# Parameter chain of the S5 layer one feed-forward earlier, its tables spread over the second, and other PSUM banks in both mixers

## The chip, the cores and the metric

The kernel runs on one core of a Trainium2 chip. A time is the device time of one execution, in microseconds; of several runs the median is given. The core has five engines with a queue each: TensorE (PE) multiplies matrices into eight PSUM banks, VectorE (DVE), ScalarE (ACT) and GpSimd (POOL) work on rows of 128 partitions, and SyncE (SP) issues the large transfers. Each queue runs in the order of the program and stops at an instruction whose operands aren't there.

## The reference

A decoder trunk of two layers on x of 256 positions by 1024. Each layer is a half-step SwiGLU, a mixer and another half-step SwiGLU, each behind an RMS norm:

```python
x = x + 0.5 * swiglu(rmsnorm(x, g0), w_gate, w_up, w_down)   # inner width 2816
x = x + mixer(rmsnorm(x, g1))
x = x + 0.5 * swiglu(rmsnorm(x, g2), w_gate, w_up, w_down)
```

The first layer's mixer is a gated spatial MLP (u, v of 512 columns each, v normed by head and mixed over positions) beside sparse attention of 8 heads (compressed, selected and windowed keys, mixed by sigmoid gates). The second layer's mixer is causal pooling beside a diagonal state-space layer (S5) of 32 groups with 64 states. What the change moves is the preparation of that layer, which depends on parameters alone:

```python
dt      = exp(log_dt)
lam_bar = exp((lam_re + 1j * lam_im) * dt)
b_bar   = ((lam_bar - 1) / lam)[..., None] * (b_re + 1j * b_im)
# states_t = lam_bar * states_{t-1} + b_bar u_t;  y = Re(c states) + d u
```

## The kernel before, in words

**Stages.** One pass in program order, in us of the profiled span: first feed-forward about 24 to 212, even mixer to 335, second feed-forward to 530, third to 722, odd mixer to 802, fourth to 1003. Activations lie with features on partitions, so a product has a weight tile as its stationary operand and 256 positions as the moving one. Each float32 weight is split into a rounded high half `wh` (ScalarE, L97) and a rest `wl` (VectorE, L98), and each product takes three matmuls: `wh` by the high half of the activation, `wl` by it, and `wh` by its low half.

**Weights.** They stream through three raw buffers of two units (a unit is 128 by 1024). `used()` marks a unit as consumed by TensorE and at once issues the split of the unit six further on. So the `wl` of a coming unit stands in VectorE's queue between the chains of the present ones, and a late VectorE makes weights late.

**A feed-forward** `ffn(f, after)` has 22 inner tiles j. A step of its loop from index 3 is: the `jobs` hung on (f, j), the projection of tile j (`proj`, 48 matmuls into `gu`, L125 to L132), `chain(j)` and the down projection of tile j-1 (24 matmuls into `y`, L114 to L116). `chain(j)` goes back and forth: `e` on VectorE (L252), `s` on ScalarE (L255), `h` on VectorE (L257), `hh` on ScalarE (L260), the low half `hl` on VectorE (L261). The projection of j+1 covers the chain of j; the last down projection follows the one before it directly. At its end `after` adds each PSUM block into x (L738) and sums squares for the next norm on GpSimd.

**Jobs** are how work of other stages gets into a feed-forward: `put(f, j0, per, todo)` hangs a list on the steps from j0, so many to a step. They are issued in program order, but GpSimd runs its own queue as fast as operands allow; only a copy called `pace` (L289), which reads `hl` of index 2, holds GpSimd back until the loop begins. Before, the jobs are:
- first feed-forward: the loads of the even mixer's constants (`even_loads`, L699), one on each step, on GpSimd's queue without a pace;
- second: the S5 parameter chain of `odd_prep` (helpers `tt`, L775, and `ts`, L779 and L781: small GpSimd instructions of 32 to 256 columns in scratch `sq`; two of its steps, a cast (L814) and a reciprocal (L861), are on VectorE, made by `with_vector`), 22 on a step; then, on the last ten steps, ten entries of the list `late`;
- third: the rest of `late`, two on a step, and in step 3 and after also the transposes `turn_w`, then the products `taps`, `cols`, `diag`, `bounce` and `phase`.

A table of `late` is one `mul2`: two products and a sum of 128 by 512 on GpSimd. Two make `bbar`, eight make `wtw`; then two scalings, a load of the C parameters, and nine more into `vt`.

**The even mixer** projects kk, q0, q1 in turn. `rope(b, o)` rotates each (four `zs`, L311, and a `zc`, L312, on VectorE, their sum on GpSimd). Then v in four units, into banks 7 and 4, and three units of narrow columns (`n`, L155: values and gate logits) into banks 6 and 5, with the attention scores of block n issued behind block n (`scores`; their row maxima are `am` on VectorE, L549, and their exponentials `pr` on ScalarE, L553, and `mu`, L347, is the mean of v's gelu). Then come twelve turns: each transposes one block of probabilities (`pt`, L571), and two or three pieces of other projections stand between as fill.

**The odd mixer** ends in `out_steps`, which accumulates the result in four banks: y[0], y[1] in 6 and 0, y[2], y[3] in 7 and 4. The first gate tile of a feed-forward is in bank 4, the next in 5 and 6.

## Time and profile before

| what | value |
|---|---|
| runs | 1007.43 us median of three, 1005.06 to 1009.93 |
| profiled execution | 1004.76 us, its span 1003.0 us |
| TensorE | busy 974.5 us, 97% |
| VectorE | busy 688.3 us, 69% |
| ScalarE | busy 477.9 us, 48% |
| GpSimd | busy 314.9 us, 31% |
| HBM read | 172 MB, 174 GB/s over the span |

An engine's busy time is the sum of its instructions in the profile; what ended an idle stretch ("releaser") is inferred from semaphores. A row of a timeline begins with start and length in us, and ends with the idle time before it and its releaser; a row of the list of windows has start and end, length, the busy time and count of TensorE's matmuls, its weight loads, VectorE, ScalarE and GpSimd, then the granted TensorE clock, the transfer engines' share and GB/s. GpSimd's work is not even: 166 of its us lie in the second feed-forward, 104 in the third, 8 in the first.

### The profile page before, as it was taken

What the parts mean: (1) busy time and instruction counts of PE and PEld (TensorE: products, weight loads), DVE (VectorE), ACT (ScalarE), POOL (GpSimd) and SP (SyncE); (2) the same over time, 40 slices, a digit from 0 to 9 for tenths busy, and PEclk for the clock granted to TensorE, in tenths of its full rate; (3) what the DMA queues carried; (4) which work ended last, traced back from release to release, by engine and by line L of the source; (5) the groups of instructions that cost most, each with busy time, mean ns of one, the idle gap of its engine ahead of it and who ended that gap; (6) DMA issues with size and microseconds to landing.
All of it is one profiled execution on the core that took longest, in us unless ns stands there. A gap on an engine that the chain in (4) does not pass through costs nothing.

```text
span 1003.0 us, 19482 instructions
## 1 busy us (share of the span) xinstructions
PE 974.5 (97%) x8171; PEld 952.8 (95%) x8171; DVE 688.3 (69%) x949; ACT 477.9 (48%) x728; POOL 314.9 (31%) x441
## 2 busy tenths in 40 slices
PE   8999999998999999999989999999999999999997
PEld 7999999998887999999989999999998999999997
DVE  6766556697774776648788788566788676656563
ACT  6544444455454564435435535444465555444442
POOL 3100000012120259999992495329510000000001
PEclk9999999997999999999998999999999999999999
DMA  8855454534212565535542745559452436554521
GB/s 280 341 210 184 180 188 173 202 138 157 85 43 84 177 247 180 188 123 198 209 167 86 273 142 184 193 181 284 173 169 119 177 133 246 191 188 175 204 85 42
DMA packets 32856, 175.48 MB, mean 175 GB/s; under 512 B 7792, under 2 KB 10032, under 8 KB 12928
## 3 DMA queue, kind: packets, MB, share of 16 engines
q1 hardware_dynamic: 29696, 166.21, 46.2%
q0 software_dynamic: 2496, 7.41, 2.4%
q8 instruction: 64, 1.05, 0.4%
q10 hardware_dynamic: 576, 0.62, 0.2%
q14 instruction: 24, 0.20, 0.1%
HBM read 172.12 MB, written 2.10 MB: 174 GB/s over the span
## 4 chain that ended last, share of the span: by engine, by line
PE 75%; POOL 9%; DVE 8%; issue 4%; ACT 3%; DMA 1%; SPq 1%; ACTq 0%; POOLq 0%; DVEq 0%
PE gu L125 13%; PE gu L127 13%; PE gu L132 13%; PE y L114 8%; PE y L116 8%; PE y L115 8%; POOL sq L775 4%; DVE wl L98 4%; POOL sq L779 3%; PE sc L541 1%; PE oT L486 1%; DMA raw<-in_ws 1%; DVE zs L311 1%; PE pt L571 1%; ACT wh L97 1%
## 5 line engine op out<-in xcount | busy, mean ns | idle before, releaser
L98 DVE TENSOR_TENSOR wl<-raw,wh 128x1024 fp32r<-128x1024 f32 x308 | 394.9, 1316 | 121.0 <-ACT wh L97 120.9
L125 PE MATMUL gu<-xh,wh 128*128 128x256 f32 x1408 | 365.5, 282 | 3.6 <-DVE x L738 2.6
L127 PE MATMUL gu<-xh,wl 128*128 128x256 f32 x1408 | 364.2, 282 | 0.6 <-DVE wl L726 0.3
L97 ACT CAST wh<-raw 128x1024 fp32r<-128x1024 f32 x308 | 311.3, 1048 | 105.4 <-PE gu L132 46.8
L132 PE MATMUL gu<-xl,wh 128*128 128x256 f32 x1408 | 275.9, 281 | 0.0
L125 PEld LDWEIGHTS gu<-xh,wh 128*128 128x128 f32 x1408 | 265.9, 189 | 5.8 <-issue 3.5
L127 PEld LDWEIGHTS gu<-xh,wl 128*128 128x128 f32 x1408 | 265.0, 188 | 1.9 <-DVE wl L726 1.7
L132 PEld LDWEIGHTS gu<-xl,wh 128*128 128x128 f32 x1408 | 213.8, 188 | 0.0
L114 PE MATMUL y<-hh,wh 128*128 128x256 f32 x704 | 199.0, 283 | 7.7 <-ACT hh L260 7.7
L116 PE MATMUL y<-hl,wh 128*128 128x256 f32 x704 | 199.4, 283 | 0.0
L115 PE MATMUL y<-hh,wl 128*128 128x256 f32 x704 | 199.2, 283 | 0.0
L255 ACT ACTIVATE s<-e 128x256 f32<-128x256 f32 x88 | 36.8, 418 | 234.7 <-DVE e L252 234.7
L114 PEld LDWEIGHTS y<-hh,wh 128*128 128x128 f32 x704 | 133.6, 190 | 8.3 <-ACT hh L260 8.3
L116 PEld LDWEIGHTS y<-hl,wh 128*128 128x128 f32 x704 | 133.4, 190 | 0.6 <-DVE hl L261 0.6
L115 PEld LDWEIGHTS y<-hh,wl 128*128 128x128 f32 x704 | 133.6, 190 | 0.0
L197 POOL TENSOR_TENSOR sq<-sq 128x512 f32<-128x512 f32 x10 | 13.6, 1360 | 292.4 <-ACT sq L195 224.5
L257 DVE TENSOR_TENSOR h<-s,e 128x256 f32<-128x256 f32 x88 | 49.5, 562 | 48.6 <-ACT s L255 48.6
L252 DVE TENSOR_TENSOR e<-gu,rb 128x512 f32<-128x512 f32 x88 | 60.5, 688 | 31.8 <-PE gu L132 30.2
L261 DVE TENSOR_TENSOR hl<-h,hh 128x256 fp32r<-128x256 f32 x88 | 41.9, 476 | 41.7 <-ACT hh L260 41.7
L747 POOL TENSOR_SCALAR sq<-x,gw 128x256 f32<-128x256 f32 x4 | 3.6, 918 | 187.0 <-DVE x L738 187.0
L260 ACT CAST hh<-h 128x256 fp32r<-128x256 f32 x88 | 35.8, 407 | 55.3 <-DVE h L257 55.3
L775 POOL TENSOR_TENSOR sq<-sq 128x64 f32<-128x64 f32 (+1 forms) x122 | 53.8, 461 | 4.0 <-DVE sq L814 0.3
(330 smaller groups left out, 1183.9 us busy)
## 6 DMA issues: line engine op xcount, KB each, us to landing
raw<-in_ws SPq DMA_DIRECT2D x154, 1024.0 KB, 4.9
toep<-kd POOLq DMA_DIRECT2D x8, 256.0 KB, 12.3
raw<-in_ws SPq DMA_DIRECT2D x4, 256.0 KB, 4.3
raw<-in_ws SPq DMA_DIRECT2D x2, 512.0 KB, 7.8
w<-in_w POOLq DMA_DIRECT2D x1, 1024.0 KB, 9.9
bnd<-in_bnd POOLq DMA_DIRECT2D x1, 544.0 KB, 9.2
x<-in_x SPq DMA_DIRECT2D x4, 128.0 KB, 3.6
x<-in_x SPq DMA_DIRECT2D x2, 256.0 KB, 7.1
```

The source lines that it names most:

```text
L97: S.copy(h, src)
L98: V.tensor_tensor(lo, src, h.bitcast(F32), op=OP.subtract)
L114: P.matmul(o, h, ah, start=first, stop=False, skip_group_check=True)
L115: P.matmul(o, lo, ah, start=False, stop=False, skip_group_check=True)
L116: P.matmul(o, h, al, start=False, stop=last, skip_group_check=True)
L125: P.matmul(os, h[:, c], xh[:, 4 * half + k], start=half == 0 and k == 0 and s == 0, stop=False, skip_group_check=True)
L127: P.matmul(os, lo[:, c], xh[:, 4 * half + k], start=False, stop=False, skip_group_check=True)
L132: P.matmul(o[:, T * s:T * s + T], h[:, c], xl[:, 4 * half + k], start=False, stop=half == 1 and k == 3, skip_group_check=True)
L252: V.tensor_tensor(e, gu[j].rearrange("p (a b) -> p a b", a=2), rb[:, None, :].to_broadcast([128, 2, T]), op=OP.mult)
L257: V.tensor_tensor(h, s, e[:, 1], op=OP.mult)
L261: V.tensor_tensor(hl[j], h, hh[j].bitcast(F32), op=OP.subtract)
L775: steps.append(lambda: G.tensor_tensor(o, p, q, op=op))
```

## The change

- The parameter chain hangs on the first feed-forward, 15 steps to a loop step instead of 22, in the same list as the even mixer's loads, and there is a `pace` copy in each of the first three feed-forwards. Its inputs `prm` and `sgn` are loaded at the start, and what it leaves (`pw`, `turn8`) lies in a pool that lives through the kernel; two results that lay in the scratch are now `turn8[3]` and `turn8[4]`.
- `late` hangs on the second feed-forward: ten entries on steps 3 to 7, three on step 8, nine on steps 10 to 18. `turn_w` is there from step 10; `cols`, `taps`, `diag`, `bounce` and `phase` are earlier in the third.
- In the even mixer the narrow block goes to banks 2 and 3, the scores n-1 follow block n, the sum of `rope(2)` is on VectorE, and v has four units of two input tiles by 512 columns, where it had two units of four input tiles for each half of 256 columns.
- In the odd mixer the banks of y[1] and y[3] change places, and the products into `yp` are in two halves with the second pooling between.

```diff
 
 def even_units():
     return (pair_units("kk", "q0") + pair_units("q1")
-            + [("v", b, k) for b in range(2) for k in range(2)] + [("n", k) for k in range(3)]
+            + [("v", k) for k in range(4)] + [("n", k) for k in range(3)]
             + pair_units("cc") + pair_units("u0") + pair_units("u1")
             + [("eo", d, k) for d, k in ((0, 0), (0, 1), (1, 0), (1, 1), (0, 2), (1, 2), (0, 3), (1, 3))])
 
...
         down(1)
         used()
         for j in range(3, NM):
-            if (f, j) in ((1, 3), (2, 3)):
+            if j == 3 and f < 3:
                 G.tensor_copy(pace, hl[j - 1].bitcast(F32)[:, 0:1])
             for job in jobs.get((f, j), ()):
                 job()
...
                 r = slice(32 * (q ^ 1), 32 * (q ^ 1) + 32)
                 V.tensor_tensor(v2(zs[32 * q:32 * q + 32]), v2(o)[r], cs[r, 1:2, :].to_broadcast([32, 2, T]), op=OP.mult)
             V.tensor_tensor(v2(zc), v2(o), cs[:, 0:1, :].to_broadcast([128, 2, T]), op=OP.mult)
-            G.tensor_tensor(roped[:, 2 * b:2 * b + 2], v2(zs), v2(zc), op=OP.add)
+            (V if b == 2 else G).tensor_tensor(roped[:, 2 * b:2 * b + 2], v2(zs), v2(zc), op=OP.add)
 
         o = [bank(4, "kk"), bank(5, "q0"), bank(6, "q1")]
         opening([("kk", o[0]), ("q0", o[1])])
...
 
         vps = [bank(7, "v0"), bank(4, "v1")]
 
-        def vblock(b, kh):
-            h, lo = unit(("v", b, kh))
-            for k in range(4):
-                c = slice(256 * k, 256 * k + 256)
-                kk = 4 * kh + k
+        def vblock(n):
+            h, lo = unit(("v", n))
+            for kk in (2 * n, 2 * n + 1):
+                c = slice(512 * (kk % 2), 512 * (kk % 2) + 512)
                 for t in range(2):
-                    mmn(vps[t][:, 256 * b:256 * b + 256], xh[:, kk, 128 * t:128 * t + 128],
-                        xl[:, kk, 128 * t:128 * t + 128], h[:, c], lo[:, c], kk == 0 and b == 0, kk == 7)
+                    mmn(vps[t], xh[:, kk, 128 * t:128 * t + 128], xl[:, kk, 128 * t:128 * t + 128], h[:, c], lo[:, c],
+                        kk == 0, kk == 7)
             used()
 
-        vblock(0, 0)
+        vblock(0)
         rope(1, o[1])
-        vblock(0, 1)
+        vblock(1)
         rope(2, o[2])
-        vblock(1, 0)
-        vblock(1, 1)
+        vblock(2)
+        vblock(3)
         gv = gm.tile([128, 8, 2, 64], F32, name="gv")
         for t in range(2):
             S.activation(gv[:, :, t], vps[t].rearrange("p (h d) -> p h d", d=64), AF.Gelu_apprx_tanh, scale=rc[:, t:t + 1])
...
             for _ in range(n):
                 next(fill, None)
 
-        nps = [bank(6, "n0"), bank(5, "n1")]
+        nps = [bank(2, "n0"), bank(3, "n1")]
         for n in range(3):
             h, lo = unit(("n", n))
             for k in range(NKS[n], NKS[n + 1]):
...
                         h[:, c], lo[:, c], k == 0, k == 7)
             if n < 2:
                 used()
-                scores(n)
+            if n:
+                scores(n - 1)
         V.tensor_scalar(hrc, rc, 0.5, None, op0=OP.mult)
         for t in range(2):
             V.tensor_scalar(vn[:, t], nps[t][:, 0:256], rc[:, t:t + 1], None, op0=OP.mult)
...
-        cr, ci = small(), small()
+        cr, ci = turn8[:, 3], turn8[:, 4]
...
         ts(turn8[:, 1], ui, sgn, OP.mult, -1.0, OP.mult)
         ts(pi, pi, sgn, OP.mult)
 
+        def put(f, j0, per, todo):
+            for i, t in enumerate(todo):
+                jobs.setdefault((f, j0 + i // per), []).append(t)
+
+        parts.append(steps)
+        j0, per = 3, 15
+        for part in parts:
+            put(0, j0, per, part)
+            j0 += -(-len(part) // per)
+        yield
+
         b1, b2 = bq[:, 0], bq[:, 1]
         g3 = lambda z: z.rearrange("p (g c) -> p g c", g=32)
         wide = lambda z: z[:, :, None].to_broadcast([128, 32, 16])
...
             late.append(lambda n=n: mul2(vt[:, :, n - 1] if n else vt0, g3(tw["c"][:, 0]), pr[:, n], g3(tw["c"][:, 1]), pi[:, n],
                                          OP.subtract))
 
-        def put(f, j0, per, todo):
-            for i, t in enumerate(todo):
-                jobs.setdefault((f, j0 + i // per), []).append(t)
-
-        parts.append(steps)
-        j0, per = 3, 22
-        for part in parts:
-            put(1, j0, per, part)
-            j0 += -(-len(part) // per)
-        put(1, NM - 10, 1, late[:10])
-        put(2, 3, 2, late[10:])
+        put(1, 3, 2, late[:10])
+        put(1, 8, 3, late[10:13])
+        put(1, 10, 1, late[13:])
 
         def turn_w(q):
             p = bank(7, "wt")
...
         scan(0)
         run(z3)
         yp = [bank(1, "yp"), bank(2, "yp")]
-        for g in range(32):
-            P.matmul(quad(yp, g), ub[:, g], tw["t"][:, g], start=g // 4 % 4 == 0, stop=False, skip_group_check=True)
-        pooled(1)
-        y = [bank(6, "y"), bank(0, "y"), None, None]
+        for hb in range(2):
+            for g in range(16 * hb, 16 * hb + 16):
+                P.matmul(quad(yp, g), ub[:, g], tw["t"][:, g], start=g // 4 % 4 == 0, stop=False, skip_group_check=True)
+            if not hb:
+                pooled(1)
+        y = [bank(6, "y"), bank(4, "y"), None, None]
 
         def out_steps(h2, k, first, last, done=None):
             h, lo = unit(("oo", h2, k))
...
         mixed_low(1, o2)
         scan(1)
         at["hold"] = False
-        y[2:] = [bank(7, "y"), bank(4, "y")]
+        y[2:] = [bank(7, "y"), bank(0, "y")]
         run(o00)
         carry(0)
         run(out_steps(1, 0, True, False))
...
+    prm = cst.tile([128, 3, 32], F32, name="prm")
+    sgn = cst.tile([128, 1], F32, name="sgn")
+    pw = cst.tile([128, 2, 9, 32], F32, name="pw")
+    turn8 = cst.tile([128, 5, 32], F32, name="turn8")
     even_loads()
+    for t_, n_ in ((prm, "prm"), (sgn, "sgn")):
+        nc.gpsimd.dma_start(t_, a[n_])
+    prep = odd_prep()
+    next(prep)
     ffn(0, step(1, 0.5))
     even(step(2, 1.0))
-    prm = ovp.tile([128, 3, 32], F32, name="prm")
-    sgn = ovp.tile([128, 1], F32, name="sgn")
-    pw = ovp.tile([128, 2, 9, 32], F32, name="pw")
-    turn8 = ovp.tile([128, 3, 32], F32, name="turn8")
...
     uu = ovp.tile([128, 32, 128], F32, tag="uu", name="uu")
     kk = ovp.tile([128, 2, 4, 128], F32, tag="kk", name="kk")
     odd_open()
-    odd_prep()
+    next(prep, None)
     ffn(1, step(3, 0.5))
     ffn(2, step(4, 0.5))
     odd(step(5, 1.0))
```

GpSimd at the first feed-forward: before, after the first norm's sum, the loads of the even mixer.

```order
L731 TENSOR_TENSOR sq<-sq 128x512 [waits Activation_49,Pool_49]
L699 DMA rot<-in_rot 128x128
L699 DMA cs<-in_cs 128x512
L699 DMA cse<-in_cse 128x64
L699 DMA neg<-in_neg 128x128
L699 DMA mc<-in_mc 128x32
```

After:

```order
L731 TENSOR_TENSOR sq<-sq 128x512 [waits Activation_49,Pool_49]
L1250 DMA prm<-in_prm 128x96
L1250 DMA sgn<-in_sgn 128x1
L289 COPY pace<-hl 128x1 [waits DVE_49]
L779 TENSOR_SCALAR sq<-prm 128x32 [waits DMASW0_49,PE_49]
L779 TENSOR_SCALAR sq<-sq 128x32 [waits Pool_49] x2
L781 TENSOR_SCALAR sq<-sq 128x32 [waits Pool_49]
```

The loads, which ran off at the start, now stand behind the pace and between the steps of the chain, the first of them some dozen steps behind it. (Rows of after carry its own line numbers.)

GpSimd at the second feed-forward, from the pace on: before, the first steps of the chain.

```order
L289 COPY pace<-hl 128x1 [waits DVE_49]
L779 TENSOR_SCALAR sq<-prm 128x32 [waits DMASW5_49,PE_49]
L779 TENSOR_SCALAR sq<-sq 128x32 [waits Pool_49] x2
L781 TENSOR_SCALAR sq<-sq 128x32 [waits Pool_49]
L779 TENSOR_SCALAR sq<-sq 128x32 [waits Pool_49]
L775 TENSOR_TENSOR sq<-sq,prm 128x32 [waits PE_49,Pool_49]
```

After, the tables (`bq` holds the B parameters, `gt` is the scratch of `mul2`):

```order
L289 COPY pace<-hl 128x1 [waits DVE_49]
L923 TENSOR_TENSOR gt<-bq,turn_198 128x512 [waits DMASW7_49]
L924 TENSOR_TENSOR gt<-bq,turn_198 128x512
L925 TENSOR_TENSOR bbar<-gt 128x512 [waits Pool_49]
L923 TENSOR_TENSOR gt<-bq,turn_198 128x512 [waits Pool_49]
L924 TENSOR_TENSOR gt<-bq,turn_198 128x512
L925 TENSOR_TENSOR bbar<-gt 128x512 [waits Pool_49]
```

Instructions of 512 columns stand where those of 32 were, and they wait for nothing but one load and one another.

VectorE in the even mixer, from the last rotation to the second maximum: before,

```order
L312 TENSOR_TENSOR zc<-q_2441,cs 128x512 [waits Pool_49]
L98 TENSOR_TENSOR wl<-raw,wh 128x1024 [waits DMAHW4_49,Activation_49]
L98 TENSOR_TENSOR wl<-raw,wh 128x1024 [waits Activation_49]
L347 TENSOR_REDUCE mu<-gv 128x16 [waits Activation_49]
L348 TENSOR_SCALAR mu<-mu 128x16 [waits DVE_49]
L98 TENSOR_TENSOR wl<-raw,wh 128x1024 [waits DMAHW5_49,PE_49,Activation_49]
L549 TENSOR_REDUCE am<-sc 128x4 [waits PE_49]
L550 TENSOR_SCALAR am<-am 128x4 [waits DVE_49]
L98 TENSOR_TENSOR wl<-raw,wh 128x1024 [waits Activation_49]
L549 TENSOR_REDUCE am<-sc 128x4 [waits PE_49]
```

After:

```order
L312 TENSOR_TENSOR zc<-q_2686,cs 128x512 [waits Pool_49]
L313 TENSOR_TENSOR roped<-zs,zc 128x512 [waits DVE_49]
L98 TENSOR_TENSOR wl<-raw,wh 128x1024 [waits DMAHW4_49,Activation_49]
L98 TENSOR_TENSOR wl<-raw,wh 128x1024 [waits Activation_49]
L346 TENSOR_REDUCE mu<-gv 128x16 [waits Activation_49]
L347 TENSOR_SCALAR mu<-mu 128x16 [waits DVE_49]
L98 TENSOR_TENSOR wl<-raw,wh 128x1024 [waits DMAHW5_49,PE_49,Activation_49]
L98 TENSOR_TENSOR wl<-raw,wh 128x1024 [waits Activation_49]
L548 TENSOR_REDUCE am<-sc 128x4 [waits PE_49]
L549 TENSOR_SCALAR am<-am 128x4 [waits DVE_49]
L548 TENSOR_REDUCE am<-sc 128x4 [waits PE_49]
```

The sum of the last rotation stands ahead of the two `wl`, and the first maximum has moved behind the second of the `wl` that stood on both sides of it.

## The prediction

> **What bounds the kernel now.** First the page's totals, then TensorE's own waits, then the stretches in which its clock was low, then VectorE, GpSimd and the chain at those places.

> ```profile
> span 1003.0 us, 19482 instructions
> PE 974.5 (97%) x8171; PEld 952.8 (95%) x8171; DVE 688.3 (69%) x949; ACT 477.9 (48%) x728; POOL 314.9 (31%) x441
> ```

> TensorE is the bound, so only what makes it wait or run slowly can be won. Its waits (total, times, longest, us):

> ```profile
> PE y L114 <- ACT hh L260: 7.7, 3, 5.0
> PE n L155 <- DVE zc L312: 3.1, 1, 3.1
> PE gu L125 <- DVE x L738: 2.6, 1, 2.6
> ```

> The 5.0 is at 522 us, in the last down projection of the second feed-forward; the 3.1 at 229 us, at the first narrow projection of the even mixer; the 2.6 at 800 us, where the last feed-forward opens. Two of them are followed by a low granted clock (column PEclk, behind the busy times):

> ```profile
> 231.80:242.00 10.20, 9.41 (x38) 8.86 (x39) 7.32 (x8) 1.30 (x2) 4.97 (x2) 0.50 0.40 157
> 525.40:532.20 6.80, 4.79 (x21) 4.53 (x22) 5.99 (x8) 2.88 (x7) 5.72 (x4) 0.50 0.27 83
> ```

> Half clock costs half of the matmul time in it: 4.7 us in the first, 2.4 us in the second.

> **The second feed-forward as it is.** VectorE's rows, two stretches:

> ```profile
> 372.75 0.69 DVE L252 TENSOR_TENSOR e<-gu,rb 128x512 f32<-128x512 f32 x1 [0.36 <-PE gu L132]
> ...
> 432.43 0.69 DVE L252 TENSOR_TENSOR e<-gu,rb 128x512 f32<-128x512 f32 x1 [0.48 <-PE gu L132]
> ...
> 446.14 0.35 DVE L861 RECIPROCAL sq<-sq 128x32 f32<-128x32 f32 x1 [9.41 <-POOL sq L775]
> ```

> ```profile
> 504.26 0.68 DVE L252 TENSOR_TENSOR e<-gu,rb 128x512 f32<-128x512 f32 x1
> 505.48 1.43 DVE L257 TENSOR_TENSOR h<-s,e 128x256 f32<-128x256 f32 x1 [0.54 <-ACT s L255]
> 507.38 0.73 DVE L261 TENSOR_TENSOR hl<-h,hh 128x256 fp32r<-128x256 f32 x1 [0.47 <-ACT hh L260]
> 508.34 6.02 DVE L98 TENSOR_TENSOR wl<-raw,wh 128x1024 fp32r<-128x1024 f32 x3 [0.23 <-ACT wh L97]
> 514.28 0.68 DVE L252 TENSOR_TENSOR e<-gu,rb 128x512 f32<-128x512 f32 x1
> ```

> From 372.75 to 432.43 GpSimd runs the small steps of the parameter chain, seven iterations take 59.7 us (8.53 each, 72 matmuls), and VectorE still waits for TensorE: the steps cost nothing. Then the reciprocal waits 9.41 us for GpSimd. From 492 us GpSimd makes tables, and an iteration of VectorE takes 10.02 us with nothing idle but ScalarE's turns; it falls 1.49 us behind in each. That is where the 5.0 comes from: TensorE resumes at

> ```profile
> 527.41 0.58 PE L114 MATMUL y<-hh,wh 128*128 128x256 f32 x1 [4.99 <-ACT hh L260]
> ```

> GpSimd's pace copy, and the first and the last of eight tables' instructions:

> ```profile
> 360.75 0.19 POOL L289 COPY pace<-hl 128x1 f32<-128x1 f32 x1 [18.60 <-DVE hl L261]
> ...
> 492.17 1.05 POOL L912 TENSOR_TENSOR gt<-bbar,pw 128x512 f32<-128x512 f32 x1
> ...
> 529.12 2.16 POOL L914 TENSOR_TENSOR wtw<-gt 128x512 f32<-128x512 f32 x1
> ```

> Eight tables in 39.1 us: 4.9 each beside TensorE's last wait, 5.0 (half of 10.02) in step with VectorE.

> **The change, part by part.**

> *Chain out of the second feed-forward.* The wait of 9.41 goes, and with it what it cost TensorE: the waits for hh are 7.7 in all and 5.0 at the longest; of the other 2.7, about half belongs to the opening of the first feed-forward and stays. I take 1.5 us (between 0 and 2.7).

> *Tables out of its end.* Ten tables start at the pace and nine more follow behind a load, some 95 us of work after 361 us, so GpSimd is done near 470. The wait of 5.0 and its half clock of 2.4 go: 7.4 us.

> *Tables into its beginning: a new wait.* They run from 361.0 to 411.2 (10 of 5.02). VectorE at that moment starts four wl (before the first chain of the loop, index 3), now 2.0 us each (6.02 for three), so e(3) comes at 369.2; TensorE's projection would let it start at 372.75-8.53 = 364.2. It is 5.0 us late. The low half hl(j) ends 3.85 us after e(j) (504.26 to 508.11), and TensorE's third matmul of that down projection needs it 8.57 us after e(j) could have started (an iteration, less the 0.2 us from the last matmul to e, and two matmuls of 0.12). So 4.7 us of lateness are free. e(3) costs 0.3, e(4) to e(6) cost 1.49 each, e(7) about 1.2 as the tables end under it: 6.0 us of new waits in pieces of up to 1.5 us. From below: 3.5, if the first four wl come through as fast as under the steps; from above: 8, if e(7) and e(8) bear the whole.
> The nine tables from about 422 to 467 start with VectorE level, and TensorE's iterations are longer there by the eight transposes moved in from the third feed-forward, where they go missing by as much; VectorE falls some 4 us back, under the 4.7: nothing. The transposes need the tables at 424 at the earliest, and these end at 411.

> *Chain into the first feed-forward.* Covered by the matmuls if it meets VectorE's reciprocal in time. The loads it is mixed with cost GpSimd 0.57 us to issue:

> ```profile
> 17.92 0.57 POOL L699 DMA_DIRECT2D cs<-in_cs  x1
> ```

> VectorE's hl that paces it, and its e of iteration 14, behind which the reciprocal now stands:

> ```profile
> 40.13 0.43 DVE L261 TENSOR_TENSOR hl<-h,hh 128x256 fp32r<-128x256 f32 x1 [0.47 <-ACT hh L260]
> ...
> 134.84 0.69 DVE L252 TENSOR_TENSOR e<-gu,rb 128x512 f32<-128x512 f32 x1 [0.49 <-PE gu L132]
> ```

> From pace to reciprocal the chain took 446.1-360.8 = 85.3 us, with VectorE as busy as here. From 40.6, and 11 loads of 0.57 on the way, it is there at 132.2; VectorE asks after 134.84 plus a chain and one wl, at 139. Cost nothing, and 7 us to spare; if that cover goes, VectorE waits, with all its wl and chains behind it, and a wait of 9.41 cost TensorE only 1.5. The rest of the chain ends some 20 us before the norm's sum needs GpSimd and the scratch. The even mixer's loads come up to 130 us later than before, still ahead of their use after 212 us.

> *Even mixer: other banks, scores one block later.* TensorE's wait of 3.1 and its half clock (4.7) would make 7.8. But what follows is a chain through VectorE, in order:

> ```profile
> 231.75 0.69 DVE L312 TENSOR_TENSOR zc<-q,cs 128x512 f32<-128x512 f32 x1
> 232.36 3.44 DVE L98 TENSOR_TENSOR wl<-raw,wh 128x1024 fp32r<-128x1024 f32 x2
> 235.72 1.21 DVE L347 TENSOR_REDUCE mu<-gv 128x16 f32<-128x1024 f32 x1
> ```

> and on the chain that ended last, maxima, table load, exponentials, a cast, and the transposes of probabilities 0 and 1:

> ```profile
> 239.71 0.70 DVE am L549
> 240.69 1.28 ACT L553
> 241.98 1.51 ACT pr L553 x8
> 243.49 0.94 ACT wh L97
> ...
> 251.30 0.92 PE pt L571 x4
> ...
> 258.00 0.82 PE pt L571 x4
> ```

> After: the addition for q1 moves to VectorE (0.7, to 233.15), two wl at 1.22 with no GpSimd beside them (235.6), mu and its scaling (237.0), two wl (239.5 to 241), two maxima (0.9 each), table load 1.3, two blocks of exponentials 3.0, the gates 0.5, a cast 1.0, a wl 1.2, and 0.75 from reciprocal to transpose: the first transpose at 248.3, 3.0 earlier. TensorE is through the narrow block, both scores and six fill steps by about 242 and idles 6 us. The 5.0 and the 3.1 both were followed by half clock, so this is too, until 252 to 256; the next transpose, which needs two fill steps and the scores between, comes at 257.2. I take 0.8 us of gain. Ends: 3.0 (clock stays) and -1.5 (half clock for the 10.2 us of the row above, from the transpose on). 512-column v blocks change only when this bubble begins: nothing.
> [...]

> *Bank 4 freed earlier in the odd mixer.* The last feed-forward's first gate tile takes bank 4, which held the last block to be added into x. Now it is bank 0. The 2.6 goes; next due is the sum of squares, 5.7+1.4 us of matmuls later, at 807:

> ```profile
> 805.22 0.43 DVE L201 TENSOR_TENSOR sq<-sq 128x256 f32<-128x256 f32 x1
> ```

> That is in time. 2.6 us (from 0, if another wait stands right behind, to 2.6). The order of yp and pooled changes no count: nothing.

> **Sum.** 1.5 + 7.4 - 6.0 + 0.8 + 2.6 = 6.3 us. The profiled execution has a span of 1003.0 and a time of 1004.76; it would be 996.7 and 998.5. The median of the runs is 1007.43, 2.7 above it; from there I predict 1001.1.

> **Rivals.**
> (a) The early tables hold no one: the four wl pass before the tables bite and the lag stays under 4.7. For it: nine such tables lie in the third feed-forward, and TensorE has no listed wait there. Against: there VectorE started level and iterations were longer. 6.0 more: 995.1.
> (b) The even mixer keeps its 7.8: the first transpose is not late, because VectorE is less of a queue than I count. Against: it has no idle gap from 224 to 238. 7.0 more: 994.1.
> (c) Gains given back: the pieces of 1.5 us lower the clock in the second feed-forward, as the 3.1 and 5.0 did. One stretch of 6.8 to 10.2 us loses 3.4 to 5.1; two of them, less the 3 us in which VectorE catches up, leave nothing: 1007. Against: the 2.6 at 800 us was followed by no such stretch.
> (d) Slower: the small steps hold VectorE in the first feed-forward as tables do. They and their loads fill some 120 us, twelve iterations. At 10.02 each that is 17.9 less 4.7, 13.2 us of waits: 1014.3. It needs 1 us per iteration to eat the gain and 1.4 to be slower by over 0.5%. Against: 372.75 to 432.43, where the excess was nothing. [...]

> **How the numbers follow.** Forecast 0.56, (a) 0.14, (b) 0.08, (c) and smaller gains 0.16, (d) 0.06. About 0.5% (5 us) is what a measurement here tells from no change. Three quarters of the forecast's own range (996 to 1005) are beyond it, so faster 0.56x0.75+0.14+0.08 = 0.64; same 0.14+0.16-0.01 = 0.29, since a little of (c) ends beyond; slower 0.07. The range takes in (a), most of (b) and most of (c): 993.5 to 1006.5.

> **What would show it.** Right: no wait near 5 us at the end of the second feed-forward and PEclk near 1 there; four or five waits of TensorE for hl or hh of about 1.5 us in its first eight iterations; wl there at 2 us; no wait of the reciprocal in the first; TensorE waiting some 6 us for pr, with half clock behind it, in the even mixer; no wait for x L738. Wrong: wl of 2 us in the first feed-forward, or the first transpose of probabilities with no wait ahead.

## The result and the profile after

The changed kernel took 999.32 us (median of four runs, 999.08 to 999.48) where the kernel before took 1007.24 (four runs, 1005.06 to 1009.93): a ratio of 0.992, interval 0.9896 to 0.9944. Measured again beside the kernel before on another chip it was 0.9945 (0.9934 to 0.9957), 999.95 against 1005.19. The profiled execution took 999.08 us. Its totals, and TensorE's longest waits (us in total, times, longest):

```profile
span 997.3 us, 19390 instructions
PE 972.1 (97%) x8123; PEld 947.3 (95%) x8123; DVE 693.9 (70%) x950; ACT 477.8 (48%) x728; POOL 317.1 (32%) x441
```

```profile
PE pt L570 <- ACT wh L97: 6.3, 1, 6.3
PE y L114 <- ACT hh L260: 4.3, 6, 1.2
...
PE y L116 <- DVE hl L261: 1.4, 6, 0.3
```

The three waits that were named are gone: the 5.0 for hh, the 3.1 for zc, the 2.6 for x. In their place stand one of 6.3 in the even mixer, and short ones for hh and hl. (The list puts the 6.3 down to a cast of ScalarE, which ended shortly before; what the transpose reads is `pr`, which VectorE scales from 248.25 us on, and the transpose starts at 248.69.) The short ones are where VectorE works beside tables (rows of VectorE, then of TensorE, in the second feed-forward):

```profile
377.90 0.68 DVE L252 TENSOR_TENSOR e<-gu,rb 128x512 f32<-128x512 f32 x1
379.12 1.43 DVE L257 TENSOR_TENSOR h<-s,e 128x256 f32<-128x256 f32 x1 [0.55 <-ACT s L255]
381.02 0.73 DVE L261 TENSOR_TENSOR hl<-h,hh 128x256 fp32r<-128x256 f32 x1 [0.47 <-ACT hh L260]
381.97 6.02 DVE L98 TENSOR_TENSOR wl<-raw,wh 128x1024 fp32r<-128x1024 f32 x3 [0.22 <-ACT wh L97]
387.91 0.68 DVE L252 TENSOR_TENSOR e<-gu,rb 128x512 f32<-128x512 f32 x1
```

```profile
381.04 0.39 PE L114 MATMUL y<-hh,wh 128*128 128x256 f32 x1 [0.71 <-ACT hh L260]
381.80 0.39 PE L116 MATMUL y<-hl,wh 128*128 128x256 f32 x1 [0.26 <-DVE hl L261]
```

An iteration of VectorE is 10.01 us, as it was at the end of this loop before, and TensorE waits for it at each down projection. The end of the loop is clean, and up to the transposes of the output half clock is now in one place only, from 245.5 us on (windows; the granted clock stands behind the five busy times):

```profile
245.50:252.30 6.80, 3.61 (x17) 3.39 (x17) 3.67 (x9) 4.59 (x7) 0.00 (x0) 0.50 0.13 25
516.00:532.00 16.00, 16.00 (x137) 16.00 (x136) 9.22 (x12) 6.61 (x9) 0.00 (x0) 1.00 0.52 194
```

By stages, from the starts of the first matmuls of each in the two traces (kk, the first gate tile of the second feed-forward, zd, the first gate tile of the fourth), us:

| execution | kk at | even mixer | second and third feed-forward | odd mixer |
|---|---|---|---|---|
| before | 200.03 | 134.71 | 392.92 | 75.08 |
| after | 199.53 | 133.89 | 391.43 | 72.53 |
| gain | 0.50 | 0.82 | 1.49 | 2.55 |

That is 5.4, and the spans differ by 5.7. The medians of the first measurement differ by 7.9. Two questions followed: where are the other 2 us, and can the two new waits be avoided?

### The profile page after: what moved, and what is told of

It is laid out like the page before. It is cut to its first block, busy times and chain, and to the rows that moved or that the text cites. A ratio compares the mean times of both kernels' runs of the same rounds, so it can differ in the third digit from the quotient of the medians.

```text
span 997.3 us, 19390 instructions
## 1 busy us (share of the span) xinstructions
PE 972.1 (97%) x8123; PEld 947.3 (95%) x8123; DVE 693.9 (70%) x950; ACT 477.8 (48%) x728; POOL 317.1 (32%) x441
## 4 chain that ended last, share of the span: by engine, by line
PE 79%; DVE 13%; ACT 4%; issue 3%; DMA 1%; SPq 1%; ACTq 0%; DVEq 0%
PE gu L125 14%; PE gu L127 14%; PE gu L132 14%; PE y L114 8%; PE y L116 8%; PE y L115 8%; DVE wl L98 7%; ACT wh L97 2%; DVE h L257 1%; PE oT L485 1%; PE sc L540 1%; DVE e L252 1%; DVE zs L311 1%; PE pt L570 1%; DMA raw<-in_ws 1%
## 5 line engine op out<-in xcount | busy, mean ns | idle before, releaser
L98 DVE TENSOR_TENSOR wl<-raw,wh 128x1024 fp32r<-128x1024 f32 x308 | 402.3, 1341 | 118.2 <-ACT wh L97 118.0
L125 PE MATMUL gu<-xh,wh 128*128 128x256 f32 x1408 | 365.7, 282 | 1.2 <-ACT wh L725 1.2
L97 ACT CAST wh<-raw 128x1024 fp32r<-128x1024 f32 x308 | 310.7, 1048 | 102.8 <-PE gu L132 44.1
L132 PE MATMUL gu<-xl,wh 128*128 128x256 f32 x1408 | 275.8, 281 | 0.0
L125 PEld LDWEIGHTS gu<-xh,wh 128*128 128x128 f32 x1408 | 266.1, 189 | 3.0 <-ACT wh L725 2.1
L132 PEld LDWEIGHTS gu<-xl,wh 128*128 128x128 f32 x1408 | 213.7, 188 | 0.0
L114 PE MATMUL y<-hh,wh 128*128 128x256 f32 x704 | 198.4, 282 | 4.3 <-ACT hh L260 4.3
L255 ACT ACTIVATE s<-e 128x256 f32<-128x256 f32 x88 | 36.8, 418 | 238.2 <-DVE e L252 238.1
L114 PEld LDWEIGHTS y<-hh,wh 128*128 128x128 f32 x704 | 132.6, 188 | 5.5 <-ACT hh L260 5.5
L197 POOL TENSOR_TENSOR sq<-sq 128x512 f32<-128x512 f32 x10 | 13.7, 1369 | 274.7 <-ACT sq L195 206.6
L252 DVE TENSOR_TENSOR e<-gu,rb 128x512 f32<-128x512 f32 x88 | 60.5, 688 | 31.3 <-PE gu L132 30.2
L257 DVE TENSOR_TENSOR h<-s,e 128x256 f32<-128x256 f32 x88 | 47.5, 540 | 48.7 <-ACT s L255 48.7
L261 DVE TENSOR_TENSOR hl<-h,hh 128x256 fp32r<-128x256 f32 x88 | 41.8, 475 | 41.8 <-ACT hh L260 41.8
L260 ACT CAST hh<-h 128x256 fp32r<-128x256 f32 x88 | 35.8, 407 | 53.4 <-DVE h L257 53.4
L775 POOL TENSOR_TENSOR sq<-sq 128x64 f32<-128x64 f32 (+1 forms) x120 | 54.4, 473 | 3.6
```

Source lines behind the costliest of these rows:

```text
L97: S.copy(h, src)
L98: V.tensor_tensor(lo, src, h.bitcast(F32), op=OP.subtract)
L114: P.matmul(o, h, ah, start=first, stop=False, skip_group_check=True)
L125: P.matmul(os, h[:, c], xh[:, 4 * half + k], start=half == 0 and k == 0 and s == 0, stop=False, skip_group_check=True)
L132: P.matmul(o[:, T * s:T * s + T], h[:, c], xl[:, 4 * half + k], start=False, stop=half == 1 and k == 3, skip_group_check=True)
L252: V.tensor_tensor(e, gu[j].rearrange("p (a b) -> p a b", a=2), rb[:, None, :].to_broadcast([128, 2, T]), op=OP.mult)
```

## The experiments

**The three parts alone, and the kernel before again.** Each part of the diff was applied to the kernel before by itself.

Odd mixer alone:

```diff
-        y = [bank(6, "y"), bank(0, "y"), None, None]
+        y = [bank(6, "y"), bank(4, "y"), None, None]
...
-        y[2:] = [bank(7, "y"), bank(4, "y")]
+        y[2:] = [bank(7, "y"), bank(0, "y")]
```

> The kernel before with the odd mixer's part alone (banks of y[1] and y[3] exchanged, yp in two halves). Theory A (each part is worth what its stage lost between the two profiled executions): 2.6 us faster than before, since the wait for x at 800 us (2.6) is gone and nothing else moves; profile's span near 1000.4. Theory B (the 2.3 us by which the medians differ more than the profiled executions belong to one wait that in some executions is followed by half clock): if that wait is this one, 5 us faster in the median, with a narrower spread.

Even mixer alone (the hunks on v, `rope`, the banks of `nps` and `scores`):

> The kernel before with the even mixer's part alone (narrow block in banks 2 and 3, scores one block later, last rotation's sum on VectorE, v by 512 columns). Theory A: 0.8 us faster, with TensorE's wait of 3.1 at the narrow block gone, a wait of about 6 ahead of the first transpose of probabilities, and the stretch of half clock moved behind it. Theory B: 3 us faster, if in other executions of before the wait of 3.1 costs a longer stretch of half clock than in the profiled one.

Feed-forwards alone (all other hunks):

> The kernel before with the parameter chain in the first feed-forward and the tables spread over the second, both mixers as before. Theory A: 1.5 us faster: 9 us of waits and half clock at the reciprocal and at the end of the second feed-forward go, some 7.4 come back as waits of TensorE for hh and hl while tables are made. Theory B: 4 us faster, if in other executions of before the wait of 5.0 at the end of the second feed-forward costs more half clock than in the profiled one.

The kernel before, with no edit:

> The kernel before once more, unchanged. Theory A: the same as before within 0.3%, and a profile with stretches of half clock after the same three waits (229, 522 and none after 800 us). Theory B: an execution nearer to the median of 1007.2 shows a further or longer stretch of half clock, after the wait at 800 us or elsewhere, worth 2 to 3 us.

| run | median us | ratio to before, interval | kk at | even | both feed-forwards | odd |
|---|---|---|---|---|---|---|
| odd alone | 1002.81 | 0.9970 (0.9961 to 0.9979) | 199.97 | 137.10 | 391.93 | 72.61 |
| even alone | 1003.92 | 0.9987 (0.9976 to 0.9997) | 199.73 | 133.83 | 391.59 | 75.04 |
| feed-forwards alone | 1004.80 | 0.9998 (0.9989 to 1.0007) | 200.41 | 135.15 | 391.92 | 74.89 |
| before again | 1005.58 | 1.0005 (0.9994 to 1.0015) | 202.58 | 136.90 | 391.85 | 75.01 |

The odd part is worth 2.5 us in every pair of executions, as expected. The even mixer as it was took 134.71, 135.15, 136.90 and 137.10 us in four executions, the changed one 133.83 and 133.89: the profiled execution of before was the shortest of its four. The two feed-forwards took 391.6 to 391.9 in the other executions of before, not 392.9. The reason for the spread is in the windows. Before again, then the feed-forwards alone:

```profile
30.00:33.40 3.40, 2.85 (x13) 2.85 (x14) 1.94 (x5) 1.72 (x4) 0.21 (x1) 0.53 1.02 426
234.80:238.20 3.40, 3.06 (x13) 3.09 (x14) 3.40 (x3) 0.00 (x0) 2.21 (x1) 0.53 0.24 99
251.90:262.10 10.20, 8.77 (x38) 8.19 (x39) 7.91 (x20) 4.32 (x12) 0.00 (x0) 0.51 0.29 104
528.30:535.20 6.90, 3.70 (x16) 3.44 (x16) 5.67 (x7) 2.13 (x4) 6.67 (x5) 0.52 0.31 131
800.00:812.00 12.00, 9.44 (x80) 9.26 (x80) 10.57 (x16) 8.45 (x15) 2.83 (x2) 1.00 0.25 89
```

```profile
233.30:236.80 3.50, 3.50 (x18) 3.45 (x16) 3.50 (x3) 0.00 (x0) 1.82 (x1) 0.54 0.06 19
250.40:253.80 3.40, 2.63 (x13) 2.59 (x14) 2.36 (x8) 2.22 (x3) 0.00 (x0) 0.53 0.00 0
803.40:806.80 3.40, 3.40 (x19) 3.40 (x18) 3.37 (x7) 3.18 (x4) 0.00 (x0) 0.53 0.00 0
```

Half clock came in stretches of 3.4 us and of two or three times that, and the same wait was followed by different numbers of them: the wait for x at 800 us by none in before, in before again and in the even part alone, by one where the feed-forwards were changed alone; the wait for zc by three (10.2 us) in before, by one in the other three executions that have it. In those three a further stretch (10.2, 10.2 and 3.4 us) stands behind a wait of 3.1 to 3.3 us ahead of the first transpose, at 250 to 253 us; in before that wait was 0.97 us, with no half clock behind it. (The 0.53 is rounding at the edges.) So what a wait cost differed from execution to execution, as the three Theories B supposed. The gains that they named for it, 5, 3 and 4 us, did not come: 3.0, 1.3 and 0.2 were measured. The kernel before, with four such places beside its opening, spread over 3 to 5 us from run to run; after, with one, over 0.4 and, measured again, over 2.

**After again.**

> The changed kernel once more, unchanged, beside a run of the kernel before on the same chip. Theory A (the three long waits of before are followed by one, two or three quanta of 3.4 us of half clock, or none, from execution to execution; after has one such place): 0.6% faster, some 6 us, about the sum of what the three parts gave alone (0.30, 0.13 and 0.02%) or a little more, and a spread of under 1 us where before has 4. Theory B (the parts help one another): 0.8%, 8 us, as first measured.

0.9945 (0.9934 to 0.9957): Theory A, except that the spread was 2 us and not under 1. The three parts alone add up to 0.45%, the whole is 0.55%; the first 0.8% had an interval that reaches to 0.56%. The stages of this execution were 133.89, 391.35 and 72.50.

**The tables one to a step.**

```diff
-            if j == 3 and f < 3:
+            if j == 3 and f < 3 or f == 1:
...
-        put(1, 3, 2, late[:10])
-        put(1, 8, 3, late[10:13])
-        put(1, 10, 1, late[13:])
+        put(1, 3, 1, late[:10])
+        put(1, 13, 3, late[10:13])
+        put(1, 13, 1, late[13:])
...
-        put(1, 10, 1, [lambda q=q: turn_w(q) for q in range(8)])
+        put(1, 14, 1, [lambda q=q: turn_w(q) for q in range(8)])
```

> The changed kernel with a pace copy in every loop step of the second feed-forward and one table to a step (ten on steps 3 to 12, nine on 13 to 21, the transposes from 14 on). Theory A (VectorE falls behind because tables run back to back beside its wl): a table of 5 us in an iteration of 8.5 leaves it level; the waits of TensorE for hh and hl between 370 and 460 us, some 7 us with their restarts, go; 7 us faster than after, about 0.992 of it. Theory B (any table in each step holds VectorE, or its hl has to wait for the pace copies that read the same buffers): no gain, or a loss of some us.

1002.05 us, 0.9961 (0.9946 to 0.9976) of before: not faster than after but 2 us slower in the median, so Theory A fell. The listed waits between 370 and 460 are gone, but the last table stands under the last chain, and the wait at the end of the loop is back:

```profile
530.93 0.50 PE L114 MATMUL y<-hh,wh 128*128 128x256 f32 x1 [3.62 <-ACT hh L260]
```

with 3.4 us of half clock behind it. The reason shows more clearly in the next kernel, which has ten tables there and none at the end.

```diff
+            if j == 3 and f < 3 or f == 1 and j < 13:
...
+        put(1, 3, 1, late[:10])
+        put(2, 3, 2, late[10:])
...
+        put(1, 14, 1, [lambda q=q: turn_w(q) for q in range(8)])
+        put(2, 11, 1, [lambda r=r: taps(r) for r in range(4)] + [diag, bounce, phase_open])
```

> The changed kernel with ten tables (bbar, wtw) on steps 3 to 12 of the second feed-forward, one to a step behind a pace copy, the transposes from step 14 on, and the nine tables vt and what follows them in the third feed-forward where the kernel before had them. Theory A (an iteration of VectorE with one table under its three wl takes 9.1 instead of 8.5; ten of them make it 6 us late at most and it catches up by the end): none of the waits of 7 us between 370 and 460, and none at the end; 7 us under after, 0.993 of it. Theory B (TensorE loses elsewhere what it no longer waits here, as the paced kernel did): less than 2 us.

997.98 us, 0.9913 (0.99 to 0.9926) of before. The two feed-forwards took 388.86, 2.5 us less than in after, not 7. No wait of TensorE is listed any more in the second, yet VectorE and TensorE go in step at 9.13 us:

```profile
398.88 6.13 DVE L98 TENSOR_TENSOR wl<-raw,wh 128x1024 fp32r<-128x1024 f32 x3 [0.46 <-ACT wh L97]
404.93 0.68 DVE L252 TENSOR_TENSOR e<-gu,rb 128x512 f32<-128x512 f32 x1
...
408.00 6.15 DVE L98 TENSOR_TENSOR wl<-raw,wh 128x1024 fp32r<-128x1024 f32 x3 [0.45 <-ACT wh L97]
414.07 0.68 DVE L252 TENSOR_TENSOR e<-gu,rb 128x512 f32<-128x512 f32 x1
```

The pace copy waits for hl, and so each table starts just when the three wl start and slows all three, 6.13 us instead of the 3.50 of three without a table (at 453.64): one table made an iteration of 9.13 us where two, running free, made one of 10.02. Without tables a late VectorE gets through one in 6.8 (e at 457.06 and at 463.85 in this trace), so one aligned table costs it 2.3 and two free ones 3.2. VectorE is already late at step 3 (e at 368.6, as in after at 367.9), so the 0.6 us by which each iteration is too long comes through at once, in four pieces of 0.1 to 0.2 that no list of waits shows. In the third feed-forward nine tables back to back, without the transposes that stood beside them before, cost 1.4 us, where before they cost nothing. That the transposes had covered them is likely from this, but no run varies it alone.

**The splits held back in the even mixer.**

```diff
-            if n < 2:
-                used()
...
-        used()
         S.activation(gsq, gv.rearrange("p a b c -> p (a b c)"), AF.Square)
         norm(0)
+        used(3)
```

> The changed kernel with the three used() of the narrow block moved behind norm(0), so that in the even mixer the splits of coming weights stand behind the maxima, gates and the first normalization in the queues of VectorE and ScalarE. Theory A (the wait of 6.3 us ahead of the first transpose is VectorE's and ScalarE's queue: two wl of 4.07 and casts ahead of what the transpose needs): the first transpose at about 243 instead of 248.7, the wait under 1.5 us, no half clock there; 7 us faster than after (5.5 of the wait, 3.4 of half clock, less some 2 that later transposes take back). Theory B: the splits are late for the fill that follows, TensorE waits there for wl instead; gain under 3 us.

The transpose came at 244.3 instead of 248.7, but zcv, which the next products need, now stood behind four wl (VectorE, then TensorE):

```profile
245.25 4.63 DVE L98 TENSOR_TENSOR wl<-raw,wh 128x1024 fp32r<-128x1024 f32 x4 [0.50 <-ACT wh L97]
249.80 1.38 DVE L382 TENSOR_TENSOR zcv<-cps,rb 64x512 f32<-64x512 f32 x2
```

```profile
251.24 0.72 PE L391 MATMUL hps<-zcv,w 128*128 128x68 f32 x4 [2.57 <-DVE zcv L382]
```

and 13.7 us of half clock came behind that. The median was 1000.0 us (0.9938, 0.992 to 0.9955): nothing gained, with Theory B's shape in another place than it named. The median hides two groups, three executions of 996.7 to 998.4 us and three of 1001.6 to 1001.8, and the profiled one, with its 13.7 us of half clock, is of the slower. With the paced tables as well:

> The changed kernel with both edits, the pace in every step and the splits held back. Theory A: the gains add, 14 us under after, about 985. Theory B: one of the edits gives nothing, 992.

999.52 us (0.9951, 0.9934 to 0.9967): no gain over after in the median. In its profiled execution the even mixer had the 6.8 us of half clock that it has in after, and took 133.02 us instead of 133.89, so by this one execution held splits are worth some 0.9 us where the clock is equal. Holding the three splits behind the second normalization, with the spread tables, was no better:

> The kernel of the spread tables, and the three used() of the narrow block moved behind the second normalization, so that neither the first transpose nor zcv stands behind the splits of coming weights. Theory A: the spread's 7 us, and in the even mixer a wait of about 2 us in place of 6.6 and no wait of hps for zcv, 4 to 8 more: 986 to 990. Theory B: the wait moves once more, to a projection whose wl is now late; then no better than the spread alone.

999.8 us (0.9927, 0.9911 to 0.9942), 2 us more than the spread tables alone. zcv was in time, but the third transpose waited 4.5 us for its probabilities:

```profile
263.34 0.87 PE L570 MATMUL pt<-ident,pr 128*128 128x128 f32 x3 [4.45 <-DVE pr L564]
```

So the waits move. Between 226 and 268 us they come to 6.9 us in after, 5.0 with the splits held, 4.8 with the paced tables as well, and 6.7 here. VectorE's queue alone doesn't make them: in after VectorE itself waits 3.7 us in this stretch for ScalarE, which from the first maximum on loads its table of functions (1.28 us) and makes eight exponentials and the gates:

```profile
245.78 0.19 DVE L645 TENSOR_SCALAR sg<-sg 128x48 f32<-128x48 f32 x1 [3.01 <-ACT sg L644]
246.71 1.23 DVE L98 TENSOR_TENSOR wl<-raw,wh 128x1024 fp32r<-128x1024 f32 x1 [0.74 <-ACT wh L97]
```

**The idle time filled.**

```diff
         go(6)
+        keep = bank(5, "keep")
+        for n in range(50):
+            P.matmul(keep[:, 0:T], xh[:, n % 8, 0:128], xh[:, (n + 1) % 8], start=True, stop=True, skip_group_check=True)
```

> The changed kernel with 50 matmuls of 256 columns into an unused bank in the even mixer's idle time ahead of the first transpose (their result is not read). Theory A (half clock follows the idle time of TensorE): the transpose comes when it came, at 248.7, no half clock behind it, 3 us under after. Theory B (half clock comes from something else than idle time at that place, or the matmuls delay the transpose): same time.

```profile
241.00:260.00 19.00, 18.07 (x143) 16.92 (x142) 13.85 (x39) 11.93 (x34) 0.63 (x1) 1.00 0.30 112
```

No half clock here, nor in the last kernel below, which has the same matmuls (granted clock 1.00 from 242 to 252 us): filling the idle time took it away, as Theory A has it. The even mixer took 132.40 instead of 133.89, a gain of 1.5 where 3 was expected: of the 6.8 us of half clock in after 3.1 lay in the wait itself, and only 3.7 us of matmuls ran at half speed. The run gave 998.43 us, 0.992 (0.9908 to 0.9932) of before.

**The tables in groups.** What the two table experiments seemed to teach is a budget: about 1.5 us late for an iteration with two tables, 1.7 taken back in one without.

```diff
+            if (f, j) in ((0, 3), (1, 5), (1, 8), (1, 11), (1, 14), (1, 17), (2, 3), (2, 4), (2, 8)):
                 G.tensor_copy(pace, hl[j - 1].bitcast(F32)[:, 0:1])
...
+        for n in range(5):
+            put(1, 5 + 3 * n, 2, late[2 * n:2 * n + 2])
+        put(2, 3, 3, late[10:13])
+        put(2, 4, 4, late[13:17])
+        put(2, 8, 5, late[17:])
```

(`turn_w` on steps 19 to 21 and, in the third loop, 3 to 7; `cols` from 11, `taps` from 12, `phase` from 18; with the 50 matmuls.)

> The changed kernel with the 50 matmuls of the run before last in the even mixer, and with the tables in groups that VectorE can catch up behind: two tables at a time on steps 5, 8, 11, 14 and 17 of the second feed-forward, four and five on steps 4 and 8 of the third, each group behind a pace copy; the transposes on the last three steps of the second and steps 3 to 7 of the third. Theory A (an iteration with two tables makes VectorE 1.5 us late, one without takes back 1.7, and 4.7 are free): no wait of TensorE for hh or hl over 0.3 us in either loop, the two feed-forwards 7 us shorter than in after, the even mixer 1.5; about 991. Theory B (what tables cost VectorE comes through to TensorE wherever they stand, as in the paced and the spread kernel): 996 or more.

993.84 us (992.97 to 995.0), 0.9883 (0.9865 to 0.9901) of before, the fastest kernel of this study. The two feed-forwards took 386.81, 4.6 less than in after, and the even mixer 132.46. A group of two tables, and VectorE level again an iteration later, waiting for TensorE (`e` 9.07 us after the one before it, then 7.98, so the group made it 0.5 us late and not 1.5):

```profile
373.55 6.06 DVE L98 TENSOR_TENSOR wl<-raw,wh 128x1024 fp32r<-128x1024 f32 x3 [0.53 <-ACT wh L97]
379.53 0.68 DVE L252 TENSOR_TENSOR e<-gu,rb 128x512 f32<-128x512 f32 x1
...
387.51 0.69 DVE L252 TENSOR_TENSOR e<-gu,rb 128x512 f32<-128x512 f32 x1 [0.47 <-PE gu L132]
...
396.04 0.69 DVE L252 TENSOR_TENSOR e<-gu,rb 128x512 f32<-128x512 f32 x1 [0.49 <-PE gu L132]
```

```profile
372.00:470.00 98.00, 98.00 (x830) 98.00 (x829) 73.79 (x70) 43.90 (x59) 38.74 (x28) 1.00 0.51 184
```

The 2.4 us that it misses of the expected 7 are a wait of that size in the last down projection of the third feed-forward (TensorE). Its lateness begins with a weight load (ScalarE, then VectorE):

```profile
715.88 0.39 PE L114 MATMUL y<-hh,wh 128*128 128x256 f32 x1 [2.43 <-ACT hh L260]
```

```profile
694.45 1.05 ACT L97 CAST wh<-raw 128x1024 fp32r<-128x1024 f32 x1 [5.38 <-DMA raw<-in_ws]
```

```profile
697.12 0.68 DVE L252 TENSOR_TENSOR e<-gu,rb 128x512 f32<-128x512 f32 x1
```

The load was issued at 680.9 us and took 13.5 us instead of the usual 5 (median 4.9 in before, 4.8 in after), in the time in which the eight `toep` transfers that follow `bounce` moved (the share of the transfer engines was 0.98 to 1.06 from 675 to 695 us). So this e came 12.06 us after the one before it, 3.5 late. The next iteration took back 1.6 of it, and the one after, beside the wide `phase` steps, lost 1.2 again (9.7 us). The `phase` steps alone are not the cause: in before they end later, at 716.4 instead of 714.9 us, and TensorE has no such wait. There a load took 14.0 us beside the same transfers, but ScalarE waited only 2.1 us for it. A run with these transfers moved was not made.

## Why the prediction was right, point by point

The sum was 6.3 us and the time 1001.1; measured were 7.9 with the first set of runs and 5.2 to 5.5 with the second, and 999.3. In the profiled executions the terms of both mixers came out nearly to the tenth, and the second and third feed-forward gave half of what was summed for them. The first feed-forward gave 0.5 instead of nothing, which tells nothing: where its code was not changed, kk began at 199.7 to 202.6 us. The spread of the kernel before, which had no term, moved the median: that the sum lies between the two measured gains is in part luck.

- **Chain into the first feed-forward, nothing.** Right, but the margin of 7 us was not there. GpSimd's steps and loads took 101 us from pace to reciprocal, not 92 (the same 174 steps took 92.7 us where they had taken 83.4; why, no run shows), and the reciprocal waited, against what the prediction lists as a sign of being right:

```profile
140.47 0.35 DVE L861 RECIPROCAL sq<-sq 128x32 f32<-128x32 f32 x1 [1.81 <-POOL sq L775]
```

  VectorE had 3.3 us of idle time in the iteration before it (e from 125.81 to 134.34 us), and TensorE, busy in all 18 us from 134 to 152, did not notice. Rival (d) needed VectorE's iterations to lengthen by 1.4 us; e of step 14 starts at 134.3 us, as it did (134.8).
- **Tables out of the end, 7.4; chain out of the second loop, 1.5.** The 5.3 us pause and the half clock at the end and the pause at the reciprocal are gone. But the matmuls that fell into half clock there took 4.8 us in the profiled execution and 3.8, 4.1 and 3.4 in the three others with the old tables, and the pause at the reciprocal, 1.7 in the profiled execution, was about 1.0 in the others. The two terms, 8.9 together, were right for the execution that they were read from (9.1) and some 1 us high for the others (7.7 to 8.1).
- **Tables into the beginning, -6.0.** The shape was right: e(3) 5 us late, wl of 2 us, then four waits of 1.2 to 1.3 (0.98 and 0.54 between starts of matmuls that are 0.12 apart otherwise) where three of 1.5 and one of 1.2 were put. All eleven pauses over 0.4 us come to 6.2 beyond the usual 0.12. What was missed is the small change: the matmul behind each wait starts 0.22 after it instead of 0.12, 1.1 us in all. And the nine later tables, put at nothing, cost 0.85 of the 6.2 at 456 us: they began at 415.9 instead of 422, when VectorE was still late from the first ten.
- So the two feed-forwards gave 1.5 where 2.9 were summed (profiled executions), and 0.2 us alone by the runs (0.9998, from 1.1 faster to 0.7 slower): **the step that failed in size is the -6.0**, which measured -7.4, with the 1.1 of restarts and the 0.85 of the nine later tables that it lacked. Beside it stand the two gains, read from one execution that was dearer than the others. Rival (a), that early tables hold no one, is out.
- **Even mixer, 0.8.** 0.82 in the profiled executions; the first transpose came at 248.7 where 248.3 was worked out, TensorE idled 6.3 where 6 was, and half clock followed. But the profiled execution of before was the shortest of its four: against their mean (135.97) the new even mixer (133.86) is 2.1 shorter, 1.3 us (0.3 to 2.4) by the runs of the part alone. Rival (b), 7.8, needed the first transpose in time, and it waited 6.3 us. The half clock behind that wait lasted 6.83 us. With the splits held it lasted 13.7 us in this mixer, though TensorE was busy in 12.91 of them; why, no run shows.
- **Odd mixer, 2.6.** 2.5 in every execution, and the half clock that sometimes followed the wait is gone with it: 3.0 (2.1 to 3.9) by the runs. TensorE runs through:

```profile
797.26 0.28 PE L116 MATMUL y<-xl,wh 128*128 128x256 f32 x1
797.38 0.28 PE L125 MATMUL gu<-xh,wh 128*128 128x256 f32 x1
```

- **Rival (c), gains given back to the clock:** out. The waits of about 1 us in the second feed-forward have no half clock behind them in any of the five executions that have them.

## What to carry to other kernels

Here a helper engine's work that slowed a second engine had a price per piece, 1.6 to 2.3 us for a table, and moving it paid where the second engine had slack between the pieces: the two feed-forwards took 391.4 us with the tables back to back, 388.9 with ten of them one to a step and 386.8 with groups and room to catch up. So look for that slack before moving such work. The pace copy, which waits on the end of a chain, aligned the helper with whatever that engine did next; a table so aligned cost VectorE 2.3 us, and 1.6 where two ran free in one iteration. And one profiled execution shows one draw of the clock: behind the waits of 2.6 to 5.0 us in the kernel before stood none to three stretches of half clock, so compare several executions stage by stage before a term is read from one.

## What was not expected of the hardware

Laid on this grid, the fourteen traces have 23 beginnings of half clock from 20 us to the end of the last feed-forward. Each stands behind a unit in which TensorE had no matmul for 1.95 us or more (2.29 and 2.94 in before, 3.21 in after), and no unit with 1.83 us or less was followed by one (1.67 at the wait for x in before). It does not hold for the transposes of the output: in after half clock begins at 989.65 us, with TensorE busy in all of the 3.41 us ahead of it. The wait for x is 2.56 to 2.57 us long in all four executions that have it: in the three executions without half clock the grid cuts it so that at most 1.7 us lie in one unit, in the fourth 2.2. So with the same wait the cost differed with where in the unit it fell.

How long half clock lasts is not explained by this. Between 500 us and the end of the last feed-forward it ended, in all seven stretches, with the first unit that was busy throughout, or nearly so (3.29 of 3.40 us in the even part alone). In the even mixer up to three such units ran at half clock (two in before, from 235.22 to 242.05 us): behind the same wait of 2.6 us for zcv four units followed in one execution and two in another, and behind the wait of 6.3 ahead of the first transpose two in four executions and four, 13.7 us, in a fifth (spread tables).
